# GLA head norm: one fp32 product replaced by two rounded products of a split square

## The chip, the cores and the metric

The kernel runs on one core of a Trainium2 chip. The metric is the device time of one execution in microseconds. Before the change the median of three runs is 1159.6 us (1158.76 to 1160.43).

## The reference, cut to what matters

One encoder block on 1024 tokens of width 1024. The mixer has two parts side by side, eight heads of neighbourhood attention and four heads of bidirectional gated linear attention (GLA); an MLP follows. What concerns the change is the end of the GLA part, a root-mean-square norm over the 128 values of each head and token:

```
def rmsnorm(x, g):
    xf = x.astype(jnp.float32)
    y = xf * lax.rsqrt(jnp.mean(xf * xf, axis=-1, keepdims=True) + EPS)
    return (y * g.astype(jnp.float32)).astype(x.dtype)
...
    o = (fwd + bwd).astype(v.dtype).transpose(0, 2, 1, 3)
    o = rmsnorm(o, norm_g) * jax.nn.silu(r.reshape(B, T, GLA_HEADS, GLA_DV))
```

The kernel holds a head's output with the 128 values on the partitions and the tokens along the free axis. The mean over the values is therefore a sum over partitions, which it takes as a product of a 128x128 matrix of ones with the squares.

## The kernel before

Large products are done in a rounded form of fp32 (fp32r): each operand is a rounded part and a rest, and three products (high by high, high by low, low by high) make up one. Some smaller ones, the sum of the squares among them, are plain fp32 products.

The GLA stage (pool `gla`, lines 486 to 733) walks over four heads. For each head: the transposed keys (`gla_ktok`), the contributions of the chunks (`gla_contrib`), a scan over 16 chunks on VectorE (`gla_scan`), the products within chunks (`gla_within`, `gla_intra`), the gates of the next head (`gla_gates`), and then for two halves of 512 tokens each `gla_inter` (16 products, and the square of the result) and `gla_norm` (sum of squares, reciprocal root in `rstd_from`, product with the gate). In the last head the second half's sum goes to `v_last`, and its norm is finished in the attention stage (lines 938 and on).

TensorE runs in the order in which the program is written: class `Ordered` (line 118) keeps every matmul in program order. Between the steps of a head stand steps of projections, which `fill` hands out; a step is three products of 128x512. The table `GLA_FILL` (line 41) says how many steps stand at each of eleven places of each head. Place 8 lies between the two `gla_inter`, place 9 between the second `gla_inter` and the first `gla_norm`, place 10 between the two norms:

```
GLA_FILL = (
    (16, 4, 4, 3, 5, 5, 2, 3, 6, 0, 3),
    (8, 2, 4, 4, 4, 2, 3, 3, 5, 0, 4),
    (9, 4, 3, 4, 4, 4, 4, 3, 6, 0, 2),
    (13, 4, 3, 4, 5, 4, 3, 3, 3, 0, 7),
)
```

In the last head the steps have run out at place 10, although the table asks for seven.

The other engines' order is made by a planner: it gives an engine the ready instruction of highest priority, which is its place in the program, moved forward by `high_priority(offset=...)`; the squares have an offset of 200 (`SOON`). A tile takes one of the slots of its tag when its first instruction is placed, and waits if none is free. Tags that matter here: "g0" and "g1" of pool `gla` with two slots each ("g1" serves the temporaries of `rstd_from`, named `nt` and `nu`, also `vtmp`, `lm` and `qt`), and the PSUM tag "s" with two banks (`la`, `c`, `a`, later the scores).

`rstd_from` (line 244) runs ScalarE Ln (L249, `nt`), Exp (L250, `ny`), Identity (L256, `nu`), Square (L257), then VectorE L258 (`nt` times `nu`) and L259.

Of the kernel before, what the change touches and what calls it, by code (L numbers as in the profile page):

```python
# [10 lines left out]
F32 = mybir.dt.float32  # L11
F32R = mybir.dt.float32r
U32 = mybir.dt.uint32
AF = mybir.ActivationFunctionType
ALU = mybir.AluOpType
# [3 lines left out]
P = 128  # L19
D = 1024  # L20
T = 1024
H = 512
# [30 lines left out]
SOON = 200  # L53
# [21 lines left out]
def block_kernel(ctx, tc, xT, g_mix, w_in, w_z, rpb, na_mask, gu, gb, g_gla, sel_f, sel_b,  # L75
                 rst, w_out, g_ff, w1, w2, g_fin, out):
    nc = tc.nc
    V, S, DMA, G = nc.vector, nc.scalar, nc.sync, nc.gpsimd
# [14 lines left out]
    def bank(tag, name):  # L93
        return ps.tile([P, H], F32, tag=tag, name=name)
# [4 lines left out]
    ones = cst.tile([P, P], F32, tag="ones", name="ones")  # L99
# [29 lines left out]
    PE = Ordered()  # L129
# [114 lines left out]
    def rstd_from(v, scale, wk, tag, n, tmp=None, bufs=1, y=None, split=False):  # L244

        if y is None:
            y = wk.tile([P, n], F32, tag=tag + "y", name=tag + "y")
        t = wk.tile([P, n], F32, tag=tmp or tag + "t", name=tag + "t", bufs=bufs)
        S.activation(t, v, AF.Ln, bias=epsb, scale=scale * LNSH)  # L249
        S.activation(y, t, AF.Exp, bias=expb, scale=-0.5)  # L250

        u = wk.tile([P, n], F32, tag=tmp or tag + "u", name=tag + "u", bufs=bufs)
        if split:
            V.tensor_scalar(u, v, -0.5 * scale, -0.5 * EPS, op0=ALU.mult, op1=ALU.add)
        else:
            S.activation(u, v, AF.Identity, bias=epsn, scale=-0.5 * scale)  # L256
        S.activation(t, y, AF.Square)  # L257
        V.tensor_tensor(t, t, u, op=ALU.mult)  # L258
        V.scalar_tensor_tensor(y, t, 1.5, y, op0=ALU.add, op1=ALU.mult)  # L259
        return y  # L260
# [34 lines left out]
    g0 = gla_stack.enter_context(pool("gla0", R))  # L295
# [176 lines left out]
    def bias_cols(cs):  # L472
        for c in cs:
            for dl in range(3):
                o = 8 * dl + 7 - c
                DMA.dma_start(rpb1[c, :, dl, :, :], rpb[:, :, o:o + CW])
# [6 lines left out]
    with pool("gla", R) as gp:  # L483
# [42 lines left out]
        def make_masks():  # L526
            selF = gp.tile([P, 1, P], F32, tag="selF", name="selF")
            selB = gp.tile([P, 1, P], F32, tag="selB", name="selB")
            G.dma_start(selF, sel_f)
            G.dma_start(selB, sel_b)  # L530
            asb = [gp.tile([P, 4, P], F32, tag=f"asb{i}", name=f"asb{i}") for i in range(2)]
            for a in asb:
                G.memset(a, 0.0)
            masks.extend([selF, selB, asb])

        def gla_gates(h, between=0):
# [18 lines left out]
                                     0.0, op0=ALU.mult, op1=ALU.add)  # L555
            return b

        def gla_keys(h, b):

            b3 = b.rearrange("p (n c) -> p n c", c=CH)  # L560
            kD = g0.tile([P, T], F32, tag="kD", name=f"kD{h}")
            dec = gp.tile([P, NCH], F32, tag="dec", name=f"dec{h}", bufs=2)
            bl = gp.tile([P, NCH], F32, tag="bl", name=f"bl{h}")
            for (lo, hi, e) in ((0, 64, CH - 1), (64, 128, 0)):
                V.tensor_copy(bl[lo:hi, :], b3[lo:hi, :, e])
            S.activation(dec, bl, AF.Exp, scale=-1.0 / 16)
            V.tensor_tensor(kD.rearrange("p (n c) -> p n c", c=CH), b3,
                            bl.unsqueeze(2).to_broadcast([P, NCH, CH]), op=ALU.subtract)
            S.activation(kD, kD, AF.Exp, scale=1.0 / 16)
            V.tensor_tensor(kD, kD, kd[h], op=ALU.mult)  # L570
            qD = gp.tile([P, T], F32, tag="qD", name=f"qD{h}", bufs=2)
            kI = gp.tile([P, T], F32, tag="kI", name=f"kI{h}", bufs=2)
            S.activation(kI, b, AF.Exp, scale=1.0 / 16)
            V.tensor_tensor(kI, kI, kd[h], op=ALU.mult)
            S.activation(qD, b, AF.Exp, scale=-1.0 / 16)
            V.tensor_tensor(qD, qD, qd[h], op=ALU.mult)
            return dec, kD, qD, kI

        def gla_ktok(h, kD):

            kt = g0.tile([P, NCH // 2, P], F32, tag="kt", name=f"kt{h}", bufs=2)
            for hf in range(2):
                tb = bank("t", f"kt{h}_{hf}")
                for i in range(4):
                    j = hf * 4 + i
                    PE.transpose(tb[:, i * P:(i + 1) * P], kD[:, j * P:(j + 1) * P], ident)
                S.copy(kt[:, hf * 4:(hf + 1) * 4, :], tb.rearrange("p (a b) -> p a b", a=4))

            st = gp.tile([P, NCH, P], F32, tag="st", name=f"st{h}")
            G.memset(st[0:64, 0, :], 0.0)  # L590
            G.memset(st[64:128, NCH - 1, :], 0.0)
            return kt, st
# [35 lines left out]
        def gla_forward(dec, st, i):  # L628
            return V.scalar_tensor_tensor(st[0:64, i + 1, :], st[0:64, i, :], dec[0:64, i:i + 1],
                                          st[0:64, i + 1, :], op0=ALU.mult, op1=ALU.add)  # L630

        def gla_scan(dec, st, i0, i1):
            for i in range(i0, i1):
                if i >= AHEAD:
                    tc.keep_in_program_order(gla_forward(dec, st, i))
                j = NCH - 1 - i
                tc.keep_in_program_order(
                    V.scalar_tensor_tensor(st[64:128, j - 1, :], st[64:128, j, :], dec[64:128, j:j + 1],
                                           st[64:128, j - 1, :], op0=ALU.mult, op1=ALU.add))
# [8 lines left out]
        def gla_inter(hf, ob, st, qD):  # L648
            for i in range(8):
                n = hf * 8 + i  # L650
                PE.matmul(ob[:, i * CH:(i + 1) * CH], st[:, n, :], qD[:, n * CH:(n + 1) * CH],
                          start=False, stop=i == 7, skip_group_check=True)
            sq = gp.tile([P, H], F32, tag="g0", name="osq", bufs=2)
            with tc.high_priority(offset=SOON):
                S.activation(sq, ob, AF.Square)
            return sq

        def gla_norm(h, hf, ob, sq):
            c = slice(hf * H, (hf + 1) * H)
            v = bank("t", f"ov{h}_{hf}")  # L660
            PE.matmul(v, ones, sq, start=True, stop=True)
            r = rstd_from(v, 1.0 / P, gp, "n", H, "g1", 2)
            if (h, hf) in gated:
                V.tensor_tensor(r, yg[h][:, c], r, op=ALU.mult)
            V.tensor_tensor(yg[h][:, c], r, ob, op=ALU.mult)
            normed.add((h, hf))
# [22 lines left out]
        for h in range(GH):  # L689
            if not masks:  # L690
                make_masks()
            fill.until(("q", h // 2))
            dec, kD, qD, kI = gla_keys(h, bs[h])
            fill.at(GLA_FILL, h, 0)
            kt, st = gla_ktok(h, kD)
            bias_cols(range(2 * h, 2 * h + 2))
            fill.at(GLA_FILL, h, 1)
            fill.until(("v", h))
            gla_contrib(h, kt, st, 0)
            for i in range(1, AHEAD):  # L700
                gla_forward(dec, st, i)
            fill.at(GLA_FILL, h, 2)
            gla_contrib(h, kt, st, 1)
            gla_scan(dec, st, 1, 5)
            fill.at(GLA_FILL, h, 3)
            gla_within(h, 0, qD, kI)
            gla_scan(dec, st, 5, 9)
            fill.at(GLA_FILL, h, 4)
            gla_within(h, 1, qD, kI)
            gla_scan(dec, st, 9, NCH - 1)  # L710
            fill.at(GLA_FILL, h, 5)
            if h + 1 < GH:
                bs[h + 1] = gla_gates(h + 1)
            ob = [gla_intra(h, 0)]
            fill.at(GLA_FILL, h, 6)
            ob.append(gla_intra(h, 1))
            fill.at(GLA_FILL, h, 7)
            sq = [gla_inter(0, ob[0], st, qD)]
            fill.at(GLA_FILL, h, 8)
            sq.append(gla_inter(1, ob[1], st, qD))  # L720
            fill.at(GLA_FILL, h, 9)
            gla_norm(h, 0, ob[0], sq[0])
            fill.at(GLA_FILL, h, 10)
            if h + 1 < GH:
                gla_norm(h, 1, ob[1], sq[1])
            else:
                v_last = bank("t", "ovlast")
                PE.matmul(v_last, ones, sq[1], start=True, stop=True)
                o_last = ob[1]
                assert (h, 1) in gated  # L730
        bias_rows(range(ROWS))
# [418 lines left out]
    def ub(name):  # L1150
        return mu.tile([P, H], F32, tag="ub", name=name, bufs=9)
# [248 lines left out]
    with tc.high_priority(offset=150):  # L1400
        for n in range(2):
            p, i = f1.order[n]
# [151 lines left out]
    for c0, n in ((H, H), (0, Q), (Q, Q)):  # L1554
        c = slice(c0, c0 + n)
        cu = slice(c0 % H, c0 % H + n)
        for d in range(NK):
# [11 lines left out]
            sq = (bank("s", "fsq") if 0 < d < own else ub("fsq"))[:, :n]  # L1569
# [98 lines left out]
```

## Time and profile before

| | |
|---|---|
| median of 3 runs | 1159.6 us |
| the profiled execution, its own time | 1158.5 us |
| its span | 1156.7 us |
| TensorE busy (PE) | 1135.4 us, 98% |
| VectorE busy (DVE) | 875.0 us, 76% |
| ScalarE busy (ACT) | 657.3 us, 57% |
| from 0 to 245 us: PE, DVE, ACT busy | 238.89, 195.10, 162.23 us |

Times in rows are microseconds from the start of the span. PE is TensorE's matmuls, PEld its weight loads, DVE is VectorE, ACT is ScalarE, POOL is GpSimd. A row of the timeline gives start, duration, engine, line, operation, output and inputs, and how many were merged; in square brackets how long the engine sat idle before and what ended that. A row by tile gives the shortest, median and longest duration in ns, then the first and last start. A row of waits gives the total, the number and the longest. Matmuls overlap in their records, so the step from start to start is what one costs.

### The profile page before, as it was taken

The page shows a single profiled execution, that of the slowest core. Times are in us where ns is not written, and L with a number is a line of the kernel's source. Part 1 is how long each engine was busy: PE and PEld are TensorE (multiplying, and loading weights), DVE is VectorE, ACT ScalarE, POOL GpSimd, SP SyncE. Part 2 cuts the span into 40 slices and gives each one's busy share as a digit, 9 for nine tenths or more (in the row PEclk, how much of TensorE's full clock was granted, in tenths as well). Part 3 has the DMA queues.
Part 4 walks back from the last instruction along what each step waited for, and adds up shares of the span by engine and source line. Part 5 has one row for each costly group of instructions (what it writes and reads, how often), then busy time and mean ns, then how long its engine had stood idle before and what let it go on. Part 6 is the DMA issues. An engine that isn't in the chain of part 4 may idle for free.

```text
span 1156.7 us, 15122 instructions
## 1 busy us (share of the span) xinstructions
PE 1135.4 (98%) x5482; PEld 928.0 (80%) x5482; DVE 875.0 (76%) x1579; ACT 657.3 (57%) x1190; POOL 242.3 (21%) x204
## 2 busy tenths in 40 slices
PE   9999999999999989999999999999999999999996
PEld 7878778778787768888788888888888888888876
DVE  7688978877676866678998976858758778587455
ACT  7758557466575655457636546446364463553665
POOL 1200000202111124500261411403214024032005
PEclk9999999999999999999999999999999999999999
DMA  7432322332322242321222012111121112111204
GB/s 245 92 95 74 76 60 52 88 74 59 73 58 66 69 182 73 109 110 38 72 73 73 25 49 74 57 53 56 55 73 37 55 55 73 55 37 55 73 1 146
DMA packets 38571, 85.07 MB, mean 74 GB/s; under 512 B 9344, under 2 KB 16640, under 8 KB 38496
## 3 DMA queue, kind: packets, MB, share of 16 engines
q1 hardware_dynamic: 34608, 71.11, 18.3%
q0 software_dynamic: 3744, 12.99, 6.2%
q8 instruction: 43, 0.70, 0.2%
q14 instruction: 32, 0.26, 0.1%
q10 hardware_dynamic: 144, 0.00, 0.0%
HBM read 79.90 MB, written 5.96 MB: 74 GB/s over the span
## 4 chain that ended last, share of the span: by engine, by line
PE 60%; DVE 2%; ACT 1%; issue 0%; DVEq 0%
PE f L122 26%; PE u L122 25%; PE op L122 7%; PE opl L122 0%; PE no L122 0%; ACT uB L1163 0%; PE vf L122 0%; ACT uB L1164 0%; DVE uB L1221 0%; DVE pl L1114 0%; PE pt L127 0%; DVE hT L1545 0%; DVE hT L1302 0%; ACT w L1513 0%; ACT u L1513 0%
## 5 line engine op out<-in xcount | busy, mean ns | idle before, releaser
L1142 ACT CAST ph<-A 128x512 fp32r<-128x512 f32 x168 | 104.3, 621 | 156.2 <-PE f L122 78.1
L1114 POOL TENSOR_TENSOR ul<-uB,uh 128x512 fp32r<-128x512 f32 x84 | 109.2, 1318 | 324.5 <-ACT uh L1155 207.5
L1114 DVE TENSOR_TENSOR pl<-A,ph 128x512 fp32r<-128x512 f32 x168 | 117.9, 713 | 53.6 <-ACT ph L1142 53.6
L122 PE MATMUL f<-uh,pl 128*128 128x512 f32 x392 | 152.6, 389 | 0.8 <-DVE pl L1114 0.8
L122 PE MATMUL f<-ul,ph 128*128 128x512 f32 x392 | 152.6, 389 | 0.0
L122 PE MATMUL f<-uh,ph 128*128 128x512 f32 x392 | 152.5, 389 | 0.0
L122 PE MATMUL proj<-nh,wh 128*128 128x512 f32 x352 | 149.6, 425 | 0.3 <-ACT wh L216 0.3
L1302 DVE TENSOR_TENSOR hT<-hT,f 128x512 f32<-128x512 f32 x196 | 131.2, 686 | 22.5 <-PE f L122 22.4
L122 PE MATMUL proj<-nh,wl 128*128 128x512 f32 x352 | 138.2, 393 | 0.0
L122 PE MATMUL proj<-nl,wh 128*128 128x512 f32 x352 | 137.6, 391 | 0.0
L122 PEld LDWEIGHTS f<-uh,pl 128*128 128x128 f32 x392 | 73.6, 188 | 16.5 <-DVE pl L1114 1.2
L122 PEld LDWEIGHTS f<-ul,ph 128*128 128x128 f32 x392 | 73.6, 188 | 15.6 <-DVE ul L1114 0.3
L122 PEld LDWEIGHTS f<-uh,ph 128*128 128x128 f32 x392 | 73.6, 188 | 15.2
L122 PE MATMUL u<-n,ph 128*128 128x512 f32 x288 | 85.2, 390 | 0.0
L1155 ACT CAST uh<-uB 128x512 fp32r<-128x512 f32 x84 | 51.9, 618 | 51.2 <-PE f L122 34.2
L122 PEld LDWEIGHTS proj<-nh,wh 128*128 128x128 f32 x352 | 66.2, 188 | 18.3 <-issue 5.0
L122 PE MATMUL op<-y,wh 128*128 128x512 f32 x240 | 76.9, 400 | 1.5 <-DVE y L751 1.3
L122 PEld LDWEIGHTS proj<-nh,wl 128*128 128x128 f32 x352 | 66.1, 188 | 15.0 <-DMA wl<-in_w_in 0.2
L122 PE MATMUL u<-T,ph 128*128 128x512 f32 x256 | 76.9, 389 | 0.0
L122 PEld LDWEIGHTS proj<-nl,wh 128*128 128x128 f32 x352 | 66.4, 189 | 11.7 <-issue 1.7
L122 PE MATMUL u<-nt,ph 128*128 128x512 f32 x224 | 69.0, 389 | 0.0
L189 POOL DMA_DIRECT2D wl<-in_w_in x21 | 18.3, 870 | 225.6 <-ACT wl L188 206.9
(322 smaller groups left out, 2419.4 us busy)
## 6 DMA issues: line engine op xcount, KB each, us to landing
A<-in_w SPq DMA_DIRECT2D x64, 512.0 KB
wf<-in_w_in SPq DMA_DIRECT2D x22, 512.0 KB
wl<-in_w_in POOLq DMA_DIRECT2D x21, 512.0 KB, 6.6
wf<-in_w_out SPq DMA_DIRECT2D x17, 512.0 KB
hT<-in_xT SPq DMA_DIRECT2D x2, 2048.0 KB
xs<-in_xT SPq DMA_DIRECT2D x8, 256.0 KB
xs<-in_xT SPq DMA_DIRECT2D x4, 512.0 KB
out<-hT SPq DMA_DIRECT2D x4, 512.0 KB
```

The source lines that it names most:

```text
L122: m = nc.tensor.matmul(*args, **kw)
L189: tc.keep_in_program_order(G.dma_start(wl, block, accum_op=ALU.add))
L1114: return kp(eng.tensor_tensor(l, x, h.bitcast(F32), op=ALU.subtract))
L1142: kp(S.copy(ph, x))
L1155: kp(S.copy(uh, x))
L1302: kp(V.tensor_tensor(hT[:, d, c], hT[:, d, c], o[:, s], op=ALU.add))
```

## The change

The square goes to a PSUM bank of tag "s" in place of an SBUF tile. ScalarE copies it to a rounded tile `sh` (tag "g0"). VectorE forms the rest, square minus rounded part, as a rounded tile `sl` (tag "g1", priority as the square). The sum over partitions is then two rounded products, of a rounded matrix of ones with `sh` and with `sl`, added up in the same PSUM bank. This is done for all eight norms; `onesr` is copied once. The table of fill steps stays as it is.

```diff
+        onesr = gp.tile([P, P], F32R, tag="onesr", name="onesr")
+        V.tensor_copy(onesr, ones)
...
-            sq = gp.tile([P, H], F32, tag="g0", name="osq", bufs=2)
+            sq = bank("s", "osq")
+            sh = gp.tile([P, H], F32R, tag="g0", name="osh", bufs=2)
             with tc.high_priority(offset=SOON):
                 S.activation(sq, ob, AF.Square)
-            return sq
+                S.copy(sh, sq)
+            return sq, sh
+
+        def ov_sum(v, sq):
+
+            sq, sh = sq
+            sl = gp.tile([P, H], F32R, tag="g1", name="osl", bufs=2)
+            with tc.high_priority(offset=SOON):
+                V.tensor_tensor(sl, sq, sh.bitcast(F32), op=ALU.subtract)
+            for i, x in enumerate((sh, sl)):
+                PE.matmul(v, onesr, x, start=i == 0, stop=i == 1)
...
             v = bank("t", f"ov{h}_{hf}")
-            PE.matmul(v, ones, sq, start=True, stop=True)
+            ov_sum(v, sq)
...
                 v_last = bank("t", "ovlast")
-                PE.matmul(v_last, ones, sq[1], start=True, stop=True)
+                ov_sum(v_last, sq[1])
```

## The prediction

> **What bounds the kernel now.** I read the page first, then the waits of the matmul engine, then the longest pieces of the chain that ended last. From the page:
>
> ```profile
> span 1156.7 us, 15122 instructions
> ...
> PE 1135.4 (98%) x5482; PEld 928.0 (80%) x5482; DVE 875.0 (76%) x1579; ACT 657.3 (57%) x1190; POOL 242.3 (21%) x204
> ...
> PE   9999999999999989999999999999999999999996
> ...
> PEclk9999999999999999999999999999999999999999
> ```
>
> PE is busy for 98% of the span, in every slice, at full granted clock. From its waits over the whole span, the longest, and those of the stage in question:
>
> ```profile
> PE la L122 <- DVE asb L625: 2.0, 1, 2.0
> ...
> PE c L122 <- ACT st L611: 0.7, 1, 0.7
> ```
>
> A wait of 2 us is the longest that there is. So a microsecond of PE work taken away or a microsecond of new PE waiting is a microsecond of the span; ACT and DVE matter only where PE waits for them. All that the change touches lies between 94 and 240 us, in the GLA stage (lines 486 to 733), where the eight norms of four heads (two halves each) stand among projection products that fill PE's time.
>
> **What is removed from PE.** From the chain that ended last, start, duration, piece:
>
> ```profile
> 454.76 19.07 PE op L122 x84
> ...
> 490.15 0.86 PE v L122 x2
> ```
>
> 84 rounded products of 128x512 follow each other in 19.07 us, 0.227 us each. One fp32 product (two records, `v`, the same shape and the same `ones` as the norm's) takes 0.86 us. The norm's own come to the same, read from the start of `ov` to the start of the second product behind it, less one step of 0.23 (the record of the first product behind starts while `ov` still runs). PE's timeline, half 0 and half 1 of heads 0 to 3:
>
> ```profile
> 99.94 1.08 PE L122 MATMUL ov<-osq,ones 128*128 128x512 f32 x2
> ...
> 102.95 1.02 PE L122 MATMUL ov<-osq,ones 128*128 128x512 f32 x2
> ...
> 104.04 0.40 PE L122 MATMUL proj<-nl,wh 128*128 128x512 f32 x1
> ...
> 143.60 1.08 PE L122 MATMUL ov<-osq,ones 128*128 128x512 f32 x2
> ...
> 147.29 1.02 PE L122 MATMUL ov<-osq,ones 128*128 128x512 f32 x2
> ...
> 148.38 0.40 PE L122 MATMUL proj<-nl,wh 128*128 128x512 f32 x1
> ...
> 190.37 1.08 PE L122 MATMUL ov<-osq,ones 128*128 128x512 f32 x2
> ...
> 192.70 1.12 PE L122 MATMUL ov<-osq,ones 128*128 128x512 f32 x2
> ...
> 193.89 0.39 PE L122 MATMUL proj<-nl,wh 128*128 128x512 f32 x1
> ...
> 234.32 1.08 PE L122 MATMUL ov<-osq,ones 128*128 128x512 f32 x2
> 235.24 1.06 PE L122 MATMUL ovlast<-osq,ones 128*128 128x512 f32 x2
> ...
> 236.37 0.39 PE L122 MATMUL proj<-nl,wh 128*128 128x512 f32 x1
> ```
>
> Half 1 of head 0: 104.04 - 0.23 - 102.95 = 0.86 us. Two rounded products cost 2 x 0.227 = 0.45. Each norm gives PE back 0.41 us, and eight give 3.3 us. That is all the change can win.
>
> **What is added.** For each half one ACT copy (PSUM to a rounded tile) and one DVE subtraction. Both kinds stand in the trace, in the same shape, with the source in PSUM (by tile `vhl`); the square is by tile `osq`:
>
> ```profile
> L836 ACT CAST vhl<-nvt x8: 577/587/592, 255.3 to 410.8; 128x512 fp32r<-128x512 f32 x8
> L837 DVE TENSOR_TENSOR vhl<-nvt,vhl x8: 680/691/692, 256.0 to 411.6; 128x512 fp32r<-128x512 f32 x8
> ...
> L655 ACT ACTIVATE osq<-o x8: 573/580/600, 96.7 to 234.5; 128x512 f32<-128x512 f32 x8
> ```
>
> Eight copies make 8 x 0.59 = 4.7 us of ACT, eight subtractions 8 x 0.69 = 5.5 us of DVE. As load neither is the bound. What counts is the way from the square to the second product. Before, it is the square alone; after, square 0.58, copy 0.59, subtraction 0.69, product 0.23, and three hand-overs, which I take at 0.05 each (`osq` of head 3 in the rows below ends at 235.12, and `ovlast` starts behind it at 235.24, so 0.12 at most): 2.25 us from the start of the square to the end of the sum. PE takes its products in program order, so the fill products behind stand still until the remainder is there.
>
> The onesr copy (128x128, once), the larger use of bank tag "s" (two free banks at that point: the next user is the contribution `c` of the next head, behind its whole first fill) and the tile in tag "g0" cost nothing that I can find; their cover is that ACT, DVE and "s" are not waited for there. Without that cover each is at most one 0.7 us operation.
>
> Half 0 has cover: after its square PE runs three to six fill steps and the inter products before `ov`. Only the second square is late. These are ACT's rows at half 1, the square and what follows it, and for head 0 one from before:
>
> ```profile
> 95.72 1.06 ACT L573 ACTIVATE kI<-b 128x1024 f32<-128x1024 f32 x1 [2.52 <-DVE b L554]
> ...
> 101.08 0.58 ACT L655 ACTIVATE osq<-o 128x512 f32<-128x512 f32 x1
> 101.56 0.62 ACT L515 ACTIVATE rtm<-rtm 128x512 f32<-128x512 f32 x1
> ...
> 145.85 0.57 ACT L655 ACTIVATE osq<-o 128x512 f32<-128x512 f32 x1
> 146.33 0.68 ACT L249 ACTIVATE nt<-ov,small 128x512 f32<-128x512 f32 x1
> 146.90 0.69 ACT L256 ACTIVATE nu<-ov,small 128x512 f32<-128x512 f32 x1
> ...
> 192.07 0.57 ACT L655 ACTIVATE osq<-o 128x512 f32<-128x512 f32 x1
> 192.59 0.63 ACT L517 ACTIVATE rtm<-rtm 128x512 f32<-128x512 f32 x1
> ...
> 234.52 0.60 ACT L655 ACTIVATE osq<-o 128x512 f32<-128x512 f32 x1 [0.17 <-PE o L122]
> 235.15 0.62 ACT L457 CAST k00p<-qt 64x512 fp32r<-64x512 f32 x1
> ```
>
> and DVE's: what it has in hand when the remainder becomes ready (heads 0 and 2), and the last use of the first half's `nu` (L258), for a rival below:
>
> ```profile
> 102.53 0.68 DVE L516 SCALAR_TENSOR_TENSOR rtm<-rtm 128x512 f32<-128x512 f32 x1
> ...
> 106.14 0.69 DVE L258 TENSOR_TENSOR nt<-nt,nu 128x512 f32<-128x512 f32 x1 [1.48 <-ACT nt L257]
> ...
> 148.89 0.69 DVE L258 TENSOR_TENSOR nt<-nt,nu 128x512 f32<-128x512 f32 x1 [1.50 <-ACT nt L257]
> ...
> 193.61 0.75 DVE L519 SCALAR_TENSOR_TENSOR yg<-rtm,ggla 128x512 f32<-128x512 f32 x1
> ```
>
> The sum of half 1 ended before at 103.81, 148.15, 193.66 and 236.14 (the next product's start less 0.23). Lower bound: squares where they are, nothing between; the end is the square's start plus 2.25, so 103.33, 148.10, 194.32, 236.77. Against before that is -0.48, -0.05, +0.66, +0.63: +0.8 us in all. The gain of half 0 is inside this, since PE now only arrives earlier at the same wait.
>
> Middle: one ready operation between square and copy. The planner gives ACT what is ready, and the copy is not ready while the square runs; the rows show `rtm`, `nt`, `rtm` and a cast right behind the four squares. Head 0: copy at 102.13 to 102.72, L516 on DVE until 103.2, remainder until 103.9, sum until 104.15 (+0.35). Head 1: copy 146.90 to 147.5, remainder until 148.2, sum until 148.5 (+0.3). Head 2: copy 193.12 to 193.7, L519 on DVE until 194.36, remainder until 195.05, sum until 195.35 (+1.7). Head 3: copy 235.77 to 236.37, remainder until 237.1, sum until 237.35 (+1.2). In all **+3.6 us**.
>
> Upper bound without a new mechanism: the half 0 copy and subtraction also push the second square back by half a microsecond at heads 0 to 2, where ACT runs on without a gap. Remainders then follow at +0.5, +1.05, +1.9 and +1.2: +4.65 us.
>
> I take the middle, since each step of it is a row. The profiled execution took 1158.5 us beside its span of 1156.7; with +3.6 it would be 1162.1. The median of the runs is 1159.6, 1.1 above, so 1163.2.
>
> [...] ACT's row at 95.72 waited 2.52 us with the square of head 0 queued behind it. [...]
>
> **Rivals.**
>
> *The slots of "g1" lock.* The remainder sl takes a slot of tag "g1", which has two, and `nt` and `nu` of half 0 take one each. If both are handed out before sl of half 1 asks, sl waits until L258 has read `nu`, and PE with it. Head 1's rows are the nearest: `nt`, `nu` follow the square directly. Sum ends would be L258's end plus 0.95: 107.8 (+4.0) at head 0 and 150.5 (+2.4) at head 1. These two in place of +0.35 and +0.3 make +9.4 us, 1169.0. Against it: sl carries the priority of 200, and if it comes between `nt` and `nu` it has the slot.
>
> [...]
>
> *The remainder keeps up: not slower.* If the plan puts square, copy and subtraction directly behind the inter products of half 1, the sum ends 2.25 us after the square starts, which can be 0.2 us after `ov` of half 0 starts (99.94, 143.60, 190.37). PE arrives 0.41 earlier than before, at 102.54, 146.88 and 192.29, so heads 0 to 2 hide all but 0.1 us and win 0.8 each; head 3 has no fill between the halves and ends at 236.77, +0.63. In all -1.85 us, 1157.7. It decides where the remainder is ready within the fill, 2.05 us at head 0 and 1.4 us at head 2. Against it: the squares stand 1.1 to 2.3 us behind `ov` of half 0 now. With the lower bound of +0.8 (1160.4) this is the group of "no difference".
>
> *Faster beyond that.* Only if head 3's wait vanishes too, 3.3 us, 1156.3; its cover of 0.45 us against 2.25 speaks against it, so it would take a luckier plan elsewhere.
>
> **How the numbers follow.** Forecast (late remainder, +2.3 to +5.5 us, 1161.9 to 1165.1): 0.46. Lock in two heads or more: 0.16. Keeps up, between -1.85 and +2.3: 0.29. Faster still: 0.09. About 0.2% (2.3 us) is what a measurement here can tell from no change: faster 0.09, same 0.29, slower 0.62. The range reaches from 1158.5 (most of "keeps up") to 1168.5 (one long lock and a part of two); the forecast's own is 1161.9 to 1165.1.
>
> **What would show it.** Right: two products of 0.227 us under `ov`; new PE waits for DVE `osl` at half 1, longest at heads 2 and 3, 0.7 to 2 us; everything after 240 us shifted by a constant. Wrong: no PE wait for `osl` (keeps up); waits of 3 us and more with DVE L258 right before `osl` (lock); PE waits that grow outside 94 to 240 us (the plan moved elsewhere).

## The result and the profile after

The change makes the kernel slower: 1184.11 us (median of 4 runs, 1183.7 to 1184.28) against 1159.28 us, a ratio of 1.0213 with a 95% interval of 1.0202 to 1.0225. The profiled execution has a span of 1182.5 us, 25.8 more than before. From the page of the changed kernel:

```profile
span 1182.5 us, 15137 instructions
...
PE 1143.0 (97%) x5482; PEld 933.7 (79%) x5482; DVE 881.6 (75%) x1588; ACT 661.3 (56%) x1198; POOL 242.0 (20%) x204
...
PE   9998989879999999999999999999999999999996
...
PEclk9998989889999999999999999999999999999999
```

The work hardly grew: DVE has 6.6 us more, ACT 4.0. But two rows changed in slices 4 to 9, the GLA stage: PE has gaps, and the granted clock (`PEclk`) dips there too. PE's waits between 85 and 300 us:

```profile
PE ov L122 <- DVE osl L668: 13.8, 4, 4.9
PE ovlast L122 <- DVE osl L668: 4.8, 1, 4.8
PE ov L122 <- ACT osh L660: 1.5, 2, 0.9
PE ovlast L122 <- ACT osh L660: 1.4, 1, 1.4
PE la L122 <- DVE asb L628: 1.1, 1, 1.1
```

The sums wait 21.5 us, 18.6 of it for the rest `osl`, with up to 4.9 us at a time. The copy `osh` costs 2.9. The wait for `la` fell from 2.0 to 1.1. Head 2, half 1, in the timelines of ACT, DVE and PE after:

```profile
205.63 0.57 ACT L660 CAST osh<-osq 128x512 fp32r<-128x512 f32 x1
...
206.77 0.75 DVE L519 SCALAR_TENSOR_TENSOR yg<-rtm,ggla 128x512 f32<-128x512 f32 x1 [0.78 <-ACT rtm L517]
...
208.19 0.68 ACT L256 ACTIVATE nu<-ov,small 128x512 f32<-128x512 f32 x1
...
209.42 0.69 DVE L258 TENSOR_TENSOR nt<-nt,nu 128x512 f32<-128x512 f32 x1 [1.90 <-ACT nt L257]
210.22 0.69 DVE L668 TENSOR_TENSOR osl<-osq,osh 128x512 fp32r<-128x512 f32 x1
...
210.96 0.80 PE L122 MATMUL ov<-osl,onesr 128*128 128x512 f32 x1 [4.21 <-DVE osl L668]
```

The copy ended at 206.20 (205.63 and 0.57), and with it the last input of `osl` was there. DVE then sat idle for most of the 0.78 us ahead of L519 and for the 1.90 us ahead of L258; it made `osl` at 210.22, right behind L258, the last reader of `nu`. At heads 0 and 3 `osl` also stands directly behind L258. At head 1 `vtmp`, another tile of "g1", comes in between, and `osl` follows L259, the last reader of `nt`:

```profile
155.43 0.69 DVE L258 TENSOR_TENSOR nt<-nt,nu 128x512 f32<-128x512 f32 x1 [1.67 <-ACT nt L257]
156.23 0.69 DVE L495 TENSOR_TENSOR vtmp<-proj,rms 128x512 f32<-128x512 f32 x1
156.84 0.68 DVE L259 SCALAR_TENSOR_TENSOR ny<-nt,ny 128x512 f32<-128x512 f32 x1
157.55 0.69 DVE L668 TENSOR_TENSOR osl<-osq,osh 128x512 fp32r<-128x512 f32 x1
```

This is the order that taken slots of "g1" give, as one of the rivals had it, and it stands in all four heads. The first experiment below tests it.

The clock falls inside each of the four long waits. PE's timeline at head 0, and the four stretches of half clock from their start to their end (length, busy time and count of PE, PEld, DVE, ACT and POOL, then the granted clock, the DMA share and GB/s):

```profile
110.12 0.63 PE L122 MATMUL proj<-nh,wl 128*128 128x512 f32 x1
110.55 0.63 PE L122 MATMUL proj<-nh,wh 128*128 128x512 f32 x1
...
112.52 0.40 PE L122 MATMUL proj<-nh,wl 128*128 128x512 f32 x1
112.76 0.40 PE L122 MATMUL proj<-nh,wh 128*128 128x512 f32 x1
```

```profile
105.49:112.32 6.83, 3.64 (x9) 2.88 (x10) 3.69 (x7) 5.12 (x8) 0.86 (x1) 0.50 0.67 145
156.69:163.52 6.83, 5.22 (x12) 4.13 (x13) 2.80 (x5) 2.04 (x3) 0.00 (x0) 0.50 0.00 0
207.89:214.72 6.83, 3.76 (x9) 2.98 (x10) 4.32 (x6) 5.09 (x9) 0.00 (x0) 0.50 0.24 78
255.68:265.92 10.24, 5.67 (x13) 4.48 (x14) 6.23 (x12) 6.45 (x10) 0.00 (x0) 0.50 0.27 67
```

At half clock one projection product takes 0.43 us from start to start, with the clock back 0.24. The clock falls 0.2 to 2.5 us after PE has begun to wait for `osl`, the stretches last two or three times 3.41 us, and the clock is back 3.6 to 5.7 us after PE goes on. It fell after shorter waits too (last section).

PE's products stand in the same order in both kernels, so each can be compared with itself. Worked out from the two traces, start of the same product after less before, in us:

```
        ahead of    behind the sum   clock full   at the next
        the norms   of half 1        again        head's norms
head 0     0.2          5.65            6.9           5.2
head 1     5.2         10.9            12.9          12.9
head 2    12.9         18.1            19.4          18.55
head 3    18.55        24.9            27.1          25.8 (the end)
```

From the first to the second column the four heads lose 22.7 us. The waits are 21.5 of it, so on balance the rounded products save nothing: with the waits left out a half 1 pair takes 1.10 us to the next start, its second product at half clock, where the fp32 product took 0.86. At half clock the products behind lose another 6.7. 3.8 us come back where the old kernel waited longer than the new one (`c` and `la` behind head 0, `c` ahead of head 3) and in the attention stage. With the 0.2 at the start this is 25.8.

### The profile page after: what moved, and what is told of

It is laid out like the page before. It is cut to its first block, busy times and chain, and to the rows that moved or that the text cites. A ratio compares the mean times of both kernels' runs of the same rounds, so it can differ in the third digit from the quotient of the medians.

```text
span 1182.5 us, 15137 instructions
## 1 busy us (share of the span) xinstructions
PE 1143.0 (97%) x5482; PEld 933.7 (79%) x5482; DVE 881.6 (75%) x1588; ACT 661.3 (56%) x1198; POOL 242.0 (20%) x204
## 4 chain that ended last, share of the span: by engine, by line
PE 58%; DVE 2%; ACT 1%; issue 0%; DVEq 0%
PE f L122 25%; PE u L122 25%; PE op L122 7%; PE opl L122 0%; PE no L122 0%; ACT uB L1177 0%; PE vf L122 0%; ACT uB L1178 0%; DVE uB L1235 0%; DVE pl L1128 0%; PE pt L127 0%; DVE hT L1559 0%; DVE hT L1316 0%; ACT w L1527 0%; ACT u L1527 0%
## 5 line engine op out<-in xcount | busy, mean ns | idle before, releaser
L122 PE MATMUL proj<-nh,wl 128*128 128x512 f32 x352 | 140.8, 400 | 0.0
L122 PE MATMUL proj<-nl,wh 128*128 128x512 f32 x352 | 140.5, 399 | 0.0
```

Of the source, the lines that this page charges most:

```text
L122: m = nc.tensor.matmul(*args, **kw)
```

## The experiments

Each ratio is against runs of the kernel before that were taken in the same round.

**The slot alone.** Half 1's rest takes a slot of "g0" in place of "g1".

```diff
-        def ov_sum(v, sq):
+        def ov_sum(v, sq, tag="g1"):
...
-            sl = gp.tile([P, H], F32R, tag="g1", name="osl", bufs=2)
+            sl = gp.tile([P, H], F32R, tag=tag, name="osl", bufs=2)
...
-            ov_sum(v, sq)
+            ov_sum(v, sq, ("g1", "g0")[hf])
...
-                ov_sum(v_last, sq[1])
+                ov_sum(v_last, sq[1], "g0")
```

> Changed against the kernel after: the rest of half 1 (osl) takes a slot of tag g0, which is free by then, in place of g1; half 0 keeps g1. Same work, same products. Theory (slots): osl waited for nu and nt of half 0 to give up g1; with another slot the four PE waits of 4 to 5 us go, the half-clock stretches go with them, and what is left is the chain square, copy, subtraction at heads 2 and 3: the forecast's middle, about 1163 us (1160 to 1165). Rival (the chain itself is late because ACT and DVE are full): waits of 3 us and more stay and the time stays above 1175 us.

Measured: 1161.98 us against 1158.67, ratio 1.0025 (1.0014 to 1.0035). PE's waits between 85 and 300 us, and head 2's second sum:

```profile
PE la L122 <- DVE asb L628: 1.9, 1, 1.9
PE ovlast L122 <- ACT osh L660: 1.4, 1, 1.4
PE ov L122 <- ACT osh L660: 1.1, 2, 0.9
...
PE ov L122 <- DVE osl L668: 0.8, 3, 0.3
PE ovlast L122 <- DVE osl L668: 0.2, 1, 0.2
```

```profile
194.53 0.49 PE L122 MATMUL ov<-osh,onesr 128*128 128x512 f32 x1 [0.88 <-ACT osh L660]
195.26 0.50 PE L122 MATMUL ov<-osl,onesr 128*128 128x512 f32 x1 [0.23 <-DVE osl L668]
195.60 0.39 PE L122 MATMUL proj<-nh,wh 128*128 128x512 f32 x1
```

The waits for `osl` fall from 18.6 to 1.0 us with the same work on every engine. The slot was the cause. What stays is the lateness of the chain, 3.5 us of waits, most of it for the copy. Two half-clock stretches of 3.41 us are still there, one behind the 1.9 us wait of `la`, one behind the last sum's 1.4 us. By the starts they cost 1.6 us each:

```profile
129.95:133.36 3.41, 3.41 (x14) 3.02 (x13) 3.12 (x10) 3.41 (x7) 0.00 (x0) 0.50 0.00 0
239.18:242.59 3.41, 3.41 (x10) 2.62 (x9) 0.75 (x2) 3.41 (x7) 0.00 (x0) 0.50 0.42 121
```

**Priority.** The subtraction gets an offset of 1000.

```diff
-            with tc.high_priority(offset=SOON):
+            with tc.high_priority(offset=1000):
                 V.tensor_tensor(sl, sq, sh.bitcast(F32), op=ALU.subtract)
```

> Changed against the kernel after: the subtraction's priority offset is 1000 in place of 200. Theory (slots): priority does not help an instruction that has no slot, so osl still stands behind L258 on DVE, four PE waits of 4 to 5 us, 1184 us within 2. Rival (DVE's order): osl moves ahead, waits fall under 2 us, time towards 1163 us.

Measured: 1185.1 us, ratio 1.0226 (1.0205 to 1.0247). The waits for `osl` are the same ones:

```profile
PE ov L122 <- DVE osl L668: 13.8, 4, 4.9
PE ovlast L122 <- DVE osl L668: 4.8, 1, 4.8
```

An offset of 1000 in place of 200 does nothing for an instruction that has no slot: 18.6 us of waits with either. My argument against the lock was that very priority.

**The clock.** PE is kept busy while it waits: 16 more products ahead of each half 1 sum, whose result is overwritten.

```diff
-        def ov_sum(v, sq):
+        def ov_sum(v, sq, keep=0):
...
+            for _ in range(keep):
+                PE.matmul(v, onesr, sh, start=True, stop=True)
             for i, x in enumerate((sh, sl)):
...
-            ov_sum(v, sq)
+            ov_sum(v, sq, 16 * hf)
...
-                ov_sum(v_last, sq[1])
+                ov_sum(v_last, sq[1], 16)
```

> Changed against the kernel after: ahead of the two products of each half 1, 16 more rounded products of onesr with osh, 3.6 us at full clock, whose result is overwritten. They fill most of the wait for osl and add no wait. Theory (clock): of the 25.8 us lost some 9 are the half-clock stretches that follow each wait; with PE busy in the waits these go and the time falls by 6 to 9 us to 1175 to 1178, though PE does 14.5 us of useless work. Rival (the 9 us are a different order on ACT and DVE): no half clock effect, time 1184 us or more.

Measured: 1175.68 us, ratio 1.0148 (1.0131 to 1.0165), against 1.0213 without: 0.0065 x 1159 = 7.5 us less for 14.5 us more work. Head 0, and the stage as a window (the clock is the next to last group):

```profile
103.10 4.15 PE L122 MATMUL ov<-osh,onesr 128*128 128x512 f32 x17
108.53 0.50 PE L122 MATMUL ov<-osl,onesr 128*128 128x512 f32 x1 [1.29 <-DVE osl L668]
108.88 0.39 PE L122 MATMUL proj<-nh,wh 128*128 128x512 f32 x1
```

```profile
85.00:300.00 215.00, 206.58 (x1165) 166.91 (x1164) 165.33 (x323) 131.84 (x231) 21.65 (x26) 1.00 0.28 63
```

`osl` comes as late as ever (the sum's second product starts at 108.53, without the filling at 108.68), the clock is full throughout, and that product takes no more than 0.35 us to the next start at each half 1, where it took 0.59. So the half clock is a cost of its own. Its size fits the 6.7 us above plus some 1 us for the four slow products of the sums themselves, though the intervals of the two ratios leave room for 4 to 11 us.

**The rounded part alone.** The second product repeats `osh` and the subtraction is left out; the rest of the squares is not in the sum, and the rounded part is in it twice.

```diff
-            sl = gp.tile([P, H], F32R, tag="g1", name="osl", bufs=2)
-            with tc.high_priority(offset=SOON):
-                V.tensor_tensor(sl, sq, sh.bitcast(F32), op=ALU.subtract)
-            for i, x in enumerate((sh, sl)):
+            for i, x in enumerate((sh, sh)):
```

> Changed against the kernel after: the second product takes the rounded part again, in place of the rest, and the subtraction is left out; so the rest of the squares is not in the sum. This leaves PE's saving with the copy alone. Theory: 8 x 0.41 = 3.3 us saved, 1 to 1.5 us of waiting for the copy at heads 2 and 3 given back, no slot lock and full clock: 1157 to 1158.5 us against 1159.3. If the rounded products saved nothing: 1160 us and more.

Measured: 1160.23 us against 1158.67, ratio 1.0012 (1.0003 to 1.0021); 1157 to 1158.5 was expected, a miss. Half 0 of head 0, where nothing waits, half 1 of head 2, and the waits:

```profile
99.62 0.71 PE L122 MATMUL ov<-osh,onesr 128*128 128x512 f32 x2
100.17 0.40 PE L122 MATMUL proj<-nh,wh 128*128 128x512 f32 x1
```

```profile
194.05 0.73 PE L122 MATMUL ov<-osh,onesr 128*128 128x512 f32 x2 [0.89 <-ACT osh L660]
194.63 0.39 PE L122 MATMUL proj<-nh,wh 128*128 128x512 f32 x1
```

```profile
PE ov L122 <- ACT osh L660: 2.7, 3, 1.5
...
PE ovlast L122 <- ACT osh L660: 1.4, 1, 1.4
```

The pair takes 0.55 us, so at half 0 the saving is what it was taken for (the same products stand 0.4 us earlier behind it at heads 0, 1 and 2). But the copy alone, without any rest, is waited for 4.1 us at the half 1 sums, where 1 to 1.5 was expected. Together with the half-clock stretch that follows the last wait here (3.41 us from 236.63), copying already costs more than the rounded products give.

**Half 0 only.** Half 1 keeps its square in SBUF and the fp32 product.

```diff
+            if hf:
+                sq = gp.tile([P, H], F32, tag="g0", name="osq", bufs=2)
+                with tc.high_priority(offset=SOON):
+                    S.activation(sq, ob, AF.Square)
+                return sq, None
...
+            if sh is None:
+                PE.matmul(v, ones, sq, start=True, stop=True)
+                return
```

> Only half 0 of each head is summed by two rounded products; half 1 keeps its square in SBUF and the fp32 product. No osl of half 1 asks for g1, and half 0 has cover. In the run with the slot moved, a rounded pair behind o took 0.54 us where the fp32 product took 0.93, so 4 x 0.39 = 1.6 us saved, less at most 0.3 us of waiting for osl at head 0. Theory: -1.3 to -1.6 us against before, no PE wait for osl over 0.3 us. Rival (any extra ACT and DVE work in the stage costs PE time): no gain, within 0.5 us of before or slower.

Measured: 1158.82 us against 1159.47, ratio 1.0000 (0.9991 to 1.0009), not the -1.3 to -1.6 us expected. Head 1, DVE and PE:

```profile
142.05 1.23 DVE L570 TENSOR_TENSOR kD<-b,bl 128x1024 f32<-128x1024 f32 x1
...
143.31 0.69 DVE L676 TENSOR_TENSOR osl<-osq,osh 128x512 fp32r<-128x512 f32 x1
...
144.05 0.50 PE L122 MATMUL ov<-osl,onesr 128*128 128x512 f32 x1 [0.65 <-DVE osl L676]
```

By the same comparison of starts, half 0 wins 0.17 at head 0 and 0.39 at head 2, and loses 0.5 at head 1. At head 3 the last sum then waits 0.2 us for its square, which leaves next to nothing, and most of what head 2 won is gone behind the `c` of head 3, which waits 0.9 us, 0.2 more than before. At head 1 the copy had ended at 139.1, yet `osl` runs behind `kD` at 143.31. That `lm` of the next head's gates held "g1" until then fits the order, but no run took it away.

**Steps moved.** The slot as in the first experiment, the last half as fp32, and one, one and two projection steps between the norms of heads 0, 1 and 2, taken from the next head's first place.

```diff
-    (16, 4, 4, 3, 5, 5, 2, 3, 6, 0, 3),
-    (8, 2, 4, 4, 4, 2, 3, 3, 5, 0, 4),
-    (9, 4, 3, 4, 4, 4, 4, 3, 6, 0, 2),
-    (13, 4, 3, 4, 5, 4, 3, 3, 3, 0, 7),
+    (16, 4, 4, 3, 5, 5, 2, 3, 6, 0, 4),
+    (7, 2, 4, 4, 4, 2, 3, 3, 5, 0, 5),
+    (8, 4, 3, 4, 4, 4, 4, 3, 6, 0, 4),
+    (11, 4, 3, 4, 5, 4, 3, 3, 3, 0, 7),
```

> The slot of half 1 moved to g0, the last head's half 1 left as the fp32 product, and one, one and two projection steps (0.68 us each) moved from the start of the next head to between the two norms of heads 0, 1 and 2. Theory (the remainder is late by 0.5 to 1.1 us there and by nothing else): waits for osh and osl fall from 3.5 us to under 0.8; saving 7 x 0.4 = 2.8 us less that: -2 to -2.8 us against before. Rival (moving steps only moves the wait on to the key transposes or the scan): -0.5 us or worse, with a longer wait at kt, c or la.

Measured: 1159.13 us against 1159.47, ratio 0.9999 (0.9990 to 1.0008). The waits of the sums are nearly gone; that of `la` stays:

```profile
PE la L122 <- DVE asb L628: 2.1, 1, 2.1
PE ov L122 <- DVE osl L676: 0.9, 2, 0.6
```

The -2 to -2.8 us did not come: the starts show 0.3 us won at head 0 and 0.7 at head 2, and 1.3 lost from the norms of head 1 to those of head 2, of which the late `osl` of half 0 is 0.5.

**Heads 0 and 2.** Head 1 goes back to the fp32 product, with its old number of steps between the norms.

```diff
+            if h == 1 or (h, hf) == (GH - 1, 1):
                 (square in SBUF and fp32 product, as above)
...
-    (7, 2, 4, 4, 4, 2, 3, 3, 5, 0, 5),
-    (8, 4, 3, 4, 4, 4, 4, 3, 6, 0, 4),
+    (7, 2, 4, 4, 4, 2, 3, 3, 5, 0, 4),
+    (9, 4, 3, 4, 4, 4, 4, 3, 6, 0, 4),
```

> Two rounded products at heads 0 and 2 (both halves) and at half 0 of head 3; head 1 and the last half keep the fp32 product. One and two projection steps moved between the norms of heads 0 and 2, slot of half 1 in g0. In the run with all steps moved, PE gained 0.3 us at head 0 and 0.7 us at head 2 and lost 1.3 us at head 1, where osl of half 0 came only after lm had given up g1. Theory: with head 1 left alone the stage ends 0.8 to 1.2 us earlier than before, the median is 0.5 to 1.2 us lower, at the edge of what can be told. Rival (head 0's gain is taken back by the wait of la for the scan, head 2's by c): stage within 0.4 us of before, no difference.

Measured: 1158.1 us against 1158.82, ratio 0.9992 (0.9983 to 1.0001). The middle of it is 0.9 us, inside what was expected, but no difference is not excluded. In the profiled execution the stage does not end 0.8 to 1.2 us earlier but 0.3 later, as the rival had it. Behind the wait of `la` it had a half-clock stretch, which cost it 1.7 us there; near 415 us it had none, where the one of before has one, and it gains 0.7 us there. So part of the 0.9 us may be the clock:

```profile
128.73 0.50 PE L122 MATMUL la<-zT,guh 128*128 128x512 f32 x1 [2.06 <-DVE asb L628]
...
130.17 0.63 PE L122 MATMUL la<-zT,gul 128*128 128x512 f32 x1
```

## Why the prediction was wrong

**The direction and the bound were right.** PE sets the span, and its new waits and slow stretches add up to the loss in the table. The direction holds without the lock too: with the slot moved the kernel is still slower by 0.25%.

**The step that failed is the choice between the forecast and the rival "the slots of g1 lock".** I gave the lock in two heads or more 0.16 and priced it for heads 0 and 1 alone, +9.4 us; it came in all four, and the change cost +24.8. The prediction read the slots right, and then set against it that `osl` has the priority of 200. The priority experiment shows that this counts for nothing. The rows of before could have told more than I took from them: in heads 0 to 2 `nt` of half 1 came only behind L258 of half 0 (at head 1 behind L259), so half 1 may already have queued for the two slots. At head 2 `nu` ran 2 us after the inputs of `osl` were ready, so it is not a race on the engines that decides. That the slot had been given away in the plan is the reading that fits this and the two experiments; the plan itself is not on record.

**The size of the lock was too low**: +4.0 and +2.4 us for heads 0 and 1 were forecast, against 5.5 and 5.7 in the table, and nothing for heads 2 and 3, which lost 5.2 and 6.35. At head 1 `vtmp` had L258's slot, so `osl` ended 2.1 us behind L258 and not 0.7. The price of the lock has no half clock in it; behind the four waits it costs 1.25 to 2.2 us each. That PE had full clock in every slice was a misreading: the trace of before has one stretch of half clock, 414.56 to 417.97, which a row of tenths hides, with no wait over 0.7 us just ahead of it.

**The forecast's middle comes out roughly when the lock is taken away.** With the slot moved, from ahead of a head's norms to behind them, PE loses 0.40, 0.17, 0.74 and 1.33 us, where +0.35, +0.3, +1.7 and +1.2 were worked out: 2.6 against 3.6 in all. At head 2 the sum is off by more than half, in part because DVE did not run L519 ahead of `osl`. That the ratio of that run, 1.0025, also is 2.9 us is partly luck: by the starts the two half-clock stretches add 3.2 us, and 2.4 come back at `c`, near 415 us and before the stage. One ready operation does stand between square and copy at heads 0, 1, 2 and 3, as assumed.

**The saving of 0.41 us a norm** holds in a stream of products (a pair takes 0.54 to 0.57 us, and 0.4 us less shows in the starts). Behind a wait it does not: there `ov` with `osl` takes 0.34 us to the next start (195.26 to 195.60 with the slot moved), not 0.23, and both products of a half 1 wait. So 3.3 us was too much for the change even without a lock.

**"Half 0 has cover"** was right but for head 1, where PE waits 0.6 us for its rest.

**Copy and subtraction** take 0.57 and 0.69 us, as their rows said.

## What to carry to other kernels

When a new temporary goes into an existing tag, count who holds its slots at the moment that it is needed and what sets them free; a high priority does not create a slot (18.6 us of waits with the offset at 200 and at 1000), and on an engine whose instructions are kept in program order, as PE's are here, one missing slot stops all the work behind it. On a matmul engine that is 98% busy a stall can cost more than its own length, when the clock drops with it: here 21.5 us of waits were followed by another 6.7 us at half clock. And where the sum of a small saving is a few tenths of a microsecond per place, the copy that it needs must already have time to spare at each place: here the four half 1 sums had none.

## What was not expected of the hardware

- Half-clock stretches also followed waits much shorter than the four long ones: 1.9 us with the slot moved, 2.1 with heads 0 and 2, 1.4 at the last sum, each with a stretch of 3.41 us. The same wait of 2.0 us in the kernel before had none behind it. The traces show a part of the reason. Within one trace the changes of the clock stand on a grid: those of the changed kernel, 105.49, 112.32, 156.69, 163.52, 207.89, 214.72, 255.68 and 265.92, are whole multiples of 3.41 us apart. In the kernel before and the changed one, away from the end of the span, each fall from full clock ends a slice of this grid in which PE was busy for only 0.50 to 1.94 of 3.41 us. With the slot moved the wait of `la` lay in one slice, with PE busy for 1.36 us of it, and the clock fell. In the kernel before the same wait was cut in two at 127.84. First the row of that slice with the slot moved (the half clock behind it, 129.95 to 133.36, is shown above). Then three rows of before: the slice behind the cut, and near 415 us a slice and the half clock behind it:

```profile
126.54:129.95 3.41, 1.36 (x6) 0.61 (x5) 3.15 (x8) 0.42 (x1) 0.00 (x0) 1.00 0.28 87
```

```profile
127.84:131.25 3.41, 1.85 (x9) 1.32 (x10) 3.15 (x8) 1.18 (x3) 0.00 (x0) 1.00 0.01 2
411.14:414.56 3.42, 1.94 (x8) 1.16 (x9) 3.38 (x9) 2.45 (x10) 1.96 (x2) 1.00 0.97 331
414.56:417.97 3.41, 3.41 (x9) 2.35 (x10) 2.70 (x8) 2.03 (x6) 0.00 (x0) 0.50 1.03 399
```

Away from both ends of the span, the traces of before and of the changed kernel have four slices at full clock with PE busy for 1.80 us or less (0.50, 1.37, 1.56 and 1.80), and half clock followed all four. Of those between 1.85 and 2.4 us it followed 1.91 and 1.94, and not 1.85, 2.19, 2.36 and 2.38, so a sharp border is not shown. What ends a stretch is open as well.

- Executions of the same kernel seem to differ by this too. Of 17 runs of the kernel before in the round of the first four experiments, the 7 with a granted clock of 0.997 took 1157.6 to 1158.7 us, the 4 with 0.995 took 1159.8 to 1160.4. By an estimate from its length and its granted clock of 0.50, one stretch of 3.41 us loses 1.7 us, 0.0015 of the span (by the starts 1.6 with the slot moved), so differences of 1 to 2 us between kernels can hang on it.
- Useless products in a wait paid for themselves: 14.5 us of them made the changed kernel some 7.5 us faster.
- The first product behind a wait takes about 0.11 us more to the next start than one in a stream (0.34 with the slot moved, 195.26 to 195.60, against 0.23).
